# Strassen-style half-size products: sums of weight blocks by accumulating DMA instead of VectorE

## The chip, the core and the metric

The kernel runs on one core of one Trainium2 chip. The metric is the device time of one execution in microseconds; the median of three runs of the kernel before is 1508.66 us (1508.45 to 1508.77).

## What is computed

One layer of an encoder trunk on 512 rows of width 2048, all in float32. The input is normalised (RMS), multiplied by one large matrix `w_in` (2048 x 13312), and split into the operands of three mixers: a short gated convolution, a banded attention with eight heads and a cross-attention into 256 memory rows with four heads. Each mixer's output is gated, projected to 2048, weighted by a sigmoid gate, summed, and projected by `w_out`.

```python
h = rms_norm(x, norm_g); proj = h @ w_in
(a_b, a_c, a_x, a_z, q, k, v, b_z, mq, m_z, g_a, g_b, g_m) = split(proj)
ya = (a_b * conv3(a_c * a_x)) * silu(a_z) @ w_branch_a
yb = (band_attention(q, k, v) * silu(b_z)) @ w_branch_b
ym = (memory_attention(mq, mem_kv) * silu(m_z)) @ w_branch_m
merged = sigmoid(g_a + b0) * ya + sigmoid(g_b + b1) * yb + sigmoid(g_m + b2) * ym
out = x + merged @ w_out
```

## The kernel before, in words

**Products.** TensorE (PE) multiplies float32 data that were split into a rounded part `hi` and a remainder `lo` (type fp32r): a product is hi*hi + hi*lo + lo*hi. `split` (L182) makes the parts of a tile: ACT casts it to `hi`, then DVE subtracts to get `lo`.

**Pairs.** `pair` (L237) computes 512 rows x 1024 columns of `h @ w_in` or `merged @ w_out` by seven half-size products instead of eight (Winograd's form of Strassen's scheme). The inner dimension 2048 and the columns are halved, so the weight has blocks 11, 12, 21 and 22, and the left matrix has halves too. Products run in the order P1, P5, P6, P3, P7, P2, P4 (`ORDER`, L234); `LEFT` (L235) names the left operand of each, sums such as S1 and S2 that `Blocks.do` (L487) makes once for all pairs. There are 15 pairs: q, k, v, cx, bz, mqz, az, two for each of the gates ga, gb, gm, and two for `w_out` (o).

**Steps.** A product is cut into n = 4 steps, one for each raw tile of 128 x 2 x 512 values (512 KB) of the weight block: 12 matmuls of 512 columns. A pair has 28 steps. In `run_steps` (L123) step i issues, in this order: the loads of step i+6, the `adds` of step i, the split of step i+2, the matmuls of step i. That is the order of the instructions on each engine; when they really start is decided by the semaphores. Every wrapper `Engine` (L40) keeps its engine's instructions in the order written, and all show as line 48, so groups are read by tile names. Raw tiles come from a ring of 12; a load waits until its slot is free. `wst` holds three split tiles, so the cast for step i+2 waits for PE to have finished step i-1.

**Block sums before.** P5, P6, P7 and P4 need sums of weight blocks. The helper `sub` makes them on DVE in the raw tiles: 11 becomes 12-11, then 22-(12-11); 12 becomes 22-12; 21 becomes 21 minus the tile 11. Those are 16 subtractions of 128 x 1024 for each pair, 240 in all.

**Queues.** SP issues all weight loads and all stores of the pairs, in program order; a store that waits for its data holds back the loads behind it. ACT issues the loads of the attention heads. POOL computes the few square roots of the norms (`rstd_of`, L158) and issues no DMA.

Of the kernel before, what the change touches and what calls it, by code (L numbers as in the profile page):

```python
# [11 lines left out]
F32 = mybir.dt.float32  # L12
F32R = mybir.dt.float32r
AF = mybir.ActivationFunctionType
ALU = mybir.AluOpType
# [50 lines left out]
def trunk_layer(ctx: ExitStack, tc, x, mem, gx, gm, w_in, w_kv, bg, cw, hg, relz, w_a, w_b, w_m, w_o, out):  # L66
# [115 lines left out]
    def split(hi, lo, f):  # L182
        ACT.copy(hi, f)
        DVE.tensor_tensor(lo, f, hi.bitcast(F32), op=ALU.subtract)
# [52 lines left out]
    def pair(name, left, w, done, bias=None, addend=None):  # L237
# [6 lines left out]
        def loader(b, kh, nh, c):  # L244
            def fn():
                raw[b, c] = load(w(kh, nh, c), f"{name}_{b}{c}")
            return fn

        def sub(dst, a, b, c):
            return lambda: DVE.tensor_tensor(raw[dst, c], raw[a, c], raw[b, c], op=ALU.subtract)  # L250

        source = {"P1": "11", "P5": "11", "P6": "11", "P3": "22", "P7": "12", "P2": "21", "P4": "21"}
        key = {"P1": "X", "P5": "Z", "P6": "Y", "P3": "Z", "P7": "Y", "P2": "V", "P4": "Y"}

        def bias_of(i):
            return st8["bias"][i]

        def evac(p):
            b = ps[key[p]]
            new = lambda what: [cell(f"{what}_{name}{t}") for t in range(2)]  # L260
            if p == "P1":
                if bias is None:
                    cs["a"] = cs["b"] = new("pa")
                    for t in range(2):
                        ACT.copy(cs["a"][t], b[t])
                else:
                    cs["a"], cs["b"] = new("pa"), new("pb")
                    for t in range(2):
                        DVE.tensor_tensor(cs["a"][t], b[t], bias_of(0), op=ALU.add)
                        DVE.tensor_tensor(cs["b"][t], b[t], bias_of(1), op=ALU.add)  # L270
            if p == "P5":
                cs["f"] = new("pf")
                for t in range(2):
                    DVE.tensor_tensor(cs["f"][t], b[t], cs["b"][t], op=ALU.add)
            if p == "P6":
                cs["e"] = new("pe") if bias is None else cs["b"]
                for t in range(2):
                    DVE.tensor_tensor(cs["e"][t], b[t], cs["b"][t], op=ALU.add)
            if p == "P3":
                for t in range(2):  # L280
                    DVE.tensor_tensor(cs["e"][t], b[t], cs["e"][t], op=ALU.add)
                done(1, 0, cs["e"])
            if p == "P7":
                for t in range(2):
                    DVE.tensor_tensor(cs["f"][t], b[t], cs["f"][t], op=ALU.add)
                done(1, 2, cs["f"])
            if p == "P2":
                cs["g"] = new("pg")
                for t in range(2):
                    DVE.tensor_tensor(cs["g"][t], b[t], cs["a"][t], op=ALU.add)  # L290
                done(0, 0, cs["g"])
            if p == "P4":
                for t in range(2):
                    DVE.tensor_tensor(cs["a"][t], b[t], cs["a"][t], op=ALU.add)
                done(0, 2, cs["a"])

        for p in ORDER:
# [21 lines left out]

        for c in range(n):  # L320
            steps[s0 + c].loads.append(loader("11", 0, 0, c))
            steps[s0 + 1 + c].loads.append(loader("12", 0, 1, c))
            steps[s0 + 7 + c].loads.append(loader("22", 1, 1, c))
            steps[s0 + 19 + c].loads.append(loader("21", 1, 0, c))
            steps[s0 + c].adds.append(sub("11", "12", "11", c))
            steps[s0 + 5 + c].adds.append(sub("11", "22", "11", c))
            steps[s0 + (10, 12, 14, 16)[c]].adds.append(sub("12", "22", "12", c))
            steps[s0 + (20, 21, 22, 24)[c]].adds.append(sub("21", "21", "11", c))
        def add_last():
            for t, e in enumerate(addend()):  # L330
                DVE.tensor_tensor(cs["a"][t], cs["a"][t], e, op=ALU.add)
# [128 lines left out]
    class Blocks:  # L460
# [16 lines left out]
        def split(self, b, i, key):  # L477
            if b not in self.at:
                self.at[b] = [slot(n, f"{self.pre}{b}_{w}", (P, 8, MEM), F32R)
                              for n, w in zip(self.slots[b], ("hi", "lo"))]  # L480
            rows = slice(4 * i, 4 * i + 4)
            split(self.at[b][0][:, rows, :], self.at[b][1][:, rows, :], self.f(key, i))

        def combine(self, d, a, b, op, i):
            DVE.tensor_tensor(self.f(d, i), self.f(a, i), self.f(b, i), op=op)

        def do(self, what, i):  # L487
            if what == "s1":
                self.combine("S12", (0, 1), (1, 1), ALU.add, i)
            elif what == "s2":  # L490
                self.combine("S12", "S12", (0, 0), ALU.subtract, i)
            elif what == "s4":
                self.combine("S4", (1, 0), "S12", ALU.subtract, i)
            elif what == "s3":
                self.combine(self.s3, (0, 0), (0, 1), ALU.subtract, i)
            else:
                key = {"A11": (0, 0), "S1": "S12", "S2": "S12", "S4": "S4", "S3": self.s3, "A12": (1, 0), "A22": (1, 1)}
                self.split(what, i, key[what])
# [434 lines left out]
```

## Time and profile before

| what | value |
|---|---|
| median of 3 runs | 1508.66 us |
| the profiled execution: its own time | 1506.83 us |
| the profiled execution: span, first to last instruction | 1505.0 us |
| PE busy | 99% |
| DVE busy | 76% |
| ACT busy | 47% |
| POOL busy | 1% |
| DMA, mean over the span | 155 GB/s |

Times are of one execution; shares are of its span. PE's busy share counts pipelined matmuls whose ends are modelled. The granted clock was full (1.000) throughout, the 2.4 GHz level.

### The profile page before, as it was taken

What the parts mean: (1) busy time and instruction counts of PE and PEld (TensorE: products, weight loads), DVE (VectorE), ACT (ScalarE), POOL (GpSimd) and SP (SyncE); (2) the same over time, 40 slices, a digit from 0 to 9 for tenths busy, and PEclk for the clock granted to TensorE, in tenths of its full rate; (3) what the DMA queues carried; (4) which work ended last, traced back from release to release, by engine and by line L of the source; (5) the groups of instructions that cost most, each with busy time, mean ns of one, the idle gap of its engine ahead of it and who ended that gap; (6) DMA issues with size and microseconds to landing.
All of it is one profiled execution on the core that took longest, in us unless ns stands there. A gap on an engine that the chain in (4) does not pass through costs nothing.

```text
span 1505.0 us, 17896 instructions
## 1 busy us (share of the span) xinstructions
PE 1483.8 (99%) x6696; PEld 1200.1 (80%) x6696; DVE 1146.7 (76%) x1393; ACT 707.4 (47%) x1102; POOL 22.0 (1%) x23
## 2 busy tenths in 40 slices
PE   8999999999999999999999999999999999998998
PEld 4478888788888888888888888888887888886887
DVE  3887778677888778887877778787887464479977
ACT  3566666543445465444444444444445343354442
POOL 0000000000000000000000000000000000000000
PEclk9999999999999999999999999999999999999999
DMA  9525354363336253626446362543736666410724
GB/s 327 191 66 180 110 175 133 102 215 112 120 90 209 70 196 98 199 89 210 140 144 221 106 223 89 184 150 114 255 133 229 234 218 209 129 43 21 253 83 133
DMA packets 139190, 233.45 MB, mean 155 GB/s; under 512 B 9824, under 2 KB 35680, under 8 KB 138464
## 3 DMA queue, kind: packets, MB, share of 16 engines
q1 hardware_dynamic: 130320, 215.41, 43.7%
q10 hardware_dynamic: 8784, 16.91, 3.4%
q8 instruction: 52, 0.85, 0.2%
q14 instruction: 34, 0.28, 0.1%
HBM read 198.73 MB, written 36.17 MB: 156 GB/s over the span
## 4 chain that ended last, share of the span: by engine, by line
PE 90%; DVE 6%; ACT 1%; DMA 1%; issue 1%; POOL 0%; SPq 0%; DVEq 0%; ACTq 0%; POOLq 0%
PE ps_wb L48 6%; PE psY_gb L48 4%; PE psY_ga L48 4%; PE psY_o L48 4%; PE psY_gm L48 3%; PE ps_kv L48 3%; PE psZ_gm L48 3%; PE psZ_gb L48 3%; PE ps_wa L48 3%; PE ps_wm L48 3%; PE psZ_ga L48 3%; PE psY_k L48 2%; PE psY_cx L48 2%; PE psZ_o L48 2%; PE psY_mqz L48 2%; PE psY_bz L48 2%
## 5 line engine op out<-in xcount | busy, mean ns | idle before, releaser
L48 ACT CAST whi_o_P<-raw_o 128x1024 fp32r<-128x1024 f32 x56 | 58.8, 1054 | 85.1 <-PE psY_o L48 20.2
L48 DVE TENSOR_TENSOR wlo_gb_P<-raw_gb,whi_gb_P 128x1024 fp32r<-128x1024 f32 x56 | 68.2, 1223 | 31.7 <-ACT whi_gb_P L48 31.4
L48 DVE TENSOR_TENSOR wlo_ga_P<-raw_ga,whi_ga_P 128x1024 fp32r<-128x1024 f32 x56 | 68.2, 1223 | 30.9 <-ACT whi_ga_P L48 30.5
L48 DVE TENSOR_TENSOR wlo_gm_P<-raw_gm,whi_gm_P 128x1024 fp32r<-128x1024 f32 x56 | 68.4, 1223 | 23.2 <-ACT whi_gm_P L48 23.2
L48 DVE TENSOR_TENSOR wlo_o_P<-raw_o,whi_o_P 128x1024 fp32r<-128x1024 f32 x56 | 68.3, 1223 | 20.4 <-ACT whi_o_P L48 20.1
L48 ACT ACTIVATE p<-p,nm 128x128 f32<-128x128 f32 (+3 forms) x32 | 18.0, 564 | 107.5 <-DVE nm L48 100.9
L48 ACT CAST whi_gm_P<-raw_gm 128x1024 fp32r<-128x1024 f32 x56 | 58.7, 1051 | 20.8 <-PE psV_gm L48 5.0
L48 ACT CAST whi_ga_P<-raw_ga 128x1024 fp32r<-128x1024 f32 x56 | 58.2, 1049 | 11.4 <-PE psY_az L48 2.8
L48 ACT CAST whi_gb_P<-raw_gb 128x1024 fp32r<-128x1024 f32 x56 | 58.4, 1049 | 6.6 <-PE psY_gb L48 2.0
L48 ACT COPY p<-ptp 128x256 f32<-128x256 f32 (+3 forms) x48 | 19.6, 409 | 88.0 <-PE ptp L48 88.0
L48 PE MATMUL ps_kv<-raw_kv,mT 128*128 128x512 f32 x128 | 59.0, 615 | 1.0 <-DMA raw_kv<-in_w_kv 1.0
L48 PE MATMUL ps_wb<-whi_wb,yb_hi 128*128 128x512 f32 x128 | 50.1, 391 | 0.0
L48 PE MATMUL ps_wb<-whi_wb,yb_lo 128*128 128x512 f32 x128 | 49.8, 389 | 0.0
L48 PE MATMUL ps_wb<-wlo_wb,yb_hi 128*128 128x512 f32 x128 | 49.8, 389 | 0.0
L48 ACT CAST whi_cx_P<-raw_cx 128x1024 fp32r<-128x1024 f32 x28 | 29.5, 1055 | 42.9 <-PE psY_cx L48 13.2
L48 DVE TENSOR_TENSOR wlo_wb<-raw_wb,whi_wb 128x1024 fp32r<-128x1024 f32 x16 | 19.6, 1223 | 38.6 <-ACT whi_wb L48 38.6
L48 PEld LDWEIGHTS ps_kv<-raw_kv,mT 128*128 128x128 f32 x128 | 24.6, 198 | 29.3 <-issue 27.9
L48 DVE TENSOR_TENSOR wlo_cx_P<-raw_cx,whi_cx_P 128x1024 fp32r<-128x1024 f32 x28 | 34.3, 1224 | 17.6 <-ACT whi_cx_P L48 15.9
L48 DVE TENSOR_TENSOR wlo_mqz_P<-raw_mqz,whi_mqz_P 128x1024 fp32r<-128x1024 f32 x28 | 34.3, 1224 | 14.2 <-ACT whi_mqz_P L48 14.2
L48 DVE TENSOR_TENSOR wlo_v_P<-raw_v,whi_v_P 128x1024 fp32r<-128x1024 f32 x28 | 34.1, 1222 | 14.2 <-ACT whi_v_P L48 13.9
L48 ACT CAST whi_mqz_P<-raw_mqz 128x1024 fp32r<-128x1024 f32 x28 | 29.4, 1051 | 31.4 <-PE psZ_mqz L48 10.0
L48 ACT CAST whi_bz_P<-raw_bz 128x1024 fp32r<-128x1024 f32 x28 | 29.5, 1054 | 30.8 <-PE psZ_bz L48 7.7
(658 smaller groups left out, 4684.7 us busy)
## 6 DMA issues: line engine op xcount, KB each, us to landing
raw_ga<-in_w_in SPq DMA_DIRECT2D x32, 512.0 KB, 4.8
raw_gb<-in_w_in SPq DMA_DIRECT2D x32, 512.0 KB, 5.3
raw_gm<-in_w_in SPq DMA_DIRECT2D x32, 512.0 KB, 5.2
raw_o<-in_w_o SPq DMA_DIRECT2D x32, 512.0 KB, 6.2
raw_kv<-in_w_kv SPq DMA_DIRECT2D x16, 512.0 KB, 7.7
raw_q<-in_w_in SPq DMA_DIRECT2D x16, 512.0 KB, 3.8
raw_k<-in_w_in SPq DMA_DIRECT2D x16, 512.0 KB, 4.8
raw_v<-in_w_in SPq DMA_DIRECT2D x16, 512.0 KB, 4.6
```

Source lines behind the costliest of these rows:

```text
L48: ins = getattr(self.engine, op)(*args, **kwargs)
```

## The change

The block sums move from DVE to DMA. `plus` issues, from POOL's queue, a transfer of a weight block out of HBM that is added into the raw tile in SBUF (`accum_op=ALU.add`). Such a transfer can only add, so the algebra is written with plus signs: tile 11 becomes 11+12, then 11+12+22, and later 11+12+22+21 for P4; tile 12 becomes 12+22. To make up for the signs, S1, S2 and S3 are formed with the opposite sign, A22 is split with a factor of -1, and `evac` subtracts in two places. Blocks 12 and 22 are now first loaded for P7 and P3 alone: their loads move from steps 1 to 4 and 7 to 10 of the pair to steps 12 to 15 and 11 to 14. The 16 loads of each pair stay; 16 accumulating transfers of 512 KB come on top.

```diff
--- before.py
+++ after.py
@@ -246,10 +246,14 @@
                 raw[b, c] = load(w(kh, nh, c), f"{name}_{b}{c}")
             return fn
 
-        def sub(dst, a, b, c):
-            return lambda: DVE.tensor_tensor(raw[dst, c], raw[a, c], raw[b, c], op=ALU.subtract)
-
-        source = {"P1": "11", "P5": "11", "P6": "11", "P3": "22", "P7": "12", "P2": "21", "P4": "21"}
+        def plus(dst, kh, nh, c):
+
+            def fn():
+                src = w(kh, nh, c).rearrange("(k p) n -> p k n", p=P)
+                POOL.dma_start(raw[dst, c], src, accum_op=ALU.add)
+            return fn
+
+        source = {"P1": "11", "P5": "11", "P6": "11", "P3": "22", "P7": "12", "P2": "21", "P4": "11"}
         key = {"P1": "X", "P5": "Z", "P6": "Y", "P3": "Z", "P7": "Y", "P2": "V", "P4": "Y"}
 
         def bias_of(i):
@@ -267,15 +271,16 @@
                     cs["a"], cs["b"] = new("pa"), new("pb")
                     for t in range(2):
                         DVE.tensor_tensor(cs["a"][t], b[t], bias_of(0), op=ALU.add)
-                        DVE.tensor_tensor(cs["b"][t], b[t], bias_of(1), op=ALU.add)
+                        DVE.tensor_tensor(cs["b"][t], bias_of(1), b[t], op=ALU.subtract)
+            other, sign = (cs["a"], ALU.subtract) if bias is None else (cs["b"], ALU.add)
             if p == "P5":
                 cs["f"] = new("pf")
                 for t in range(2):
-                    DVE.tensor_tensor(cs["f"][t], b[t], cs["b"][t], op=ALU.add)
+                    DVE.tensor_tensor(cs["f"][t], b[t], other[t], op=sign)
             if p == "P6":
                 cs["e"] = new("pe") if bias is None else cs["b"]
                 for t in range(2):
-                    DVE.tensor_tensor(cs["e"][t], b[t], cs["b"][t], op=ALU.add)
+                    DVE.tensor_tensor(cs["e"][t], b[t], other[t], op=sign)
             if p == "P3":
                 for t in range(2):
                     DVE.tensor_tensor(cs["e"][t], b[t], cs["e"][t], op=ALU.add)
@@ -291,7 +296,7 @@
                 done(0, 0, cs["g"])
             if p == "P4":
                 for t in range(2):
-                    DVE.tensor_tensor(cs["a"][t], b[t], cs["a"][t], op=ALU.add)
+                    DVE.tensor_tensor(cs["a"][t], cs["a"][t], b[t], op=ALU.subtract)
                 done(0, 2, cs["a"])
 
         for p in ORDER:
@@ -319,13 +324,13 @@
 
         for c in range(n):
             steps[s0 + c].loads.append(loader("11", 0, 0, c))
-            steps[s0 + 1 + c].loads.append(loader("12", 0, 1, c))
-            steps[s0 + 7 + c].loads.append(loader("22", 1, 1, c))
+            steps[s0 + 12 + c].loads.append(loader("12", 0, 1, c))
+            steps[s0 + 11 + c].loads.append(loader("22", 1, 1, c))
             steps[s0 + 19 + c].loads.append(loader("21", 1, 0, c))
-            steps[s0 + c].adds.append(sub("11", "12", "11", c))
-            steps[s0 + 5 + c].adds.append(sub("11", "22", "11", c))
-            steps[s0 + (10, 12, 14, 16)[c]].adds.append(sub("12", "22", "12", c))
-            steps[s0 + (20, 21, 22, 24)[c]].adds.append(sub("21", "21", "11", c))
+            steps[s0 - 1 + c].adds.append(plus("11", 0, 1, c))
+            steps[s0 + 3 + c].adds.append(plus("11", 1, 1, c))
+            steps[s0 + 9 + c].adds.append(plus("12", 1, 1, c))
+            steps[s0 + 13 + c].adds.append(plus("11", 1, 0, c))
         def add_last():
             for t, e in enumerate(addend()):
                 DVE.tensor_tensor(cs["a"][t], cs["a"][t], e, op=ALU.add)
@@ -479,20 +484,26 @@
                 self.at[b] = [slot(n, f"{self.pre}{b}_{w}", (P, 8, MEM), F32R)
                               for n, w in zip(self.slots[b], ("hi", "lo"))]
             rows = slice(4 * i, 4 * i + 4)
-            split(self.at[b][0][:, rows, :], self.at[b][1][:, rows, :], self.f(key, i))
+            hi, lo, f = self.at[b][0][:, rows, :], self.at[b][1][:, rows, :], self.f(key, i)
+            if b != "A22":
+                split(hi, lo, f)
+                return
+
+            ACT.mul(hi, f, -1.0)
+            DVE.scalar_tensor_tensor(lo, f, -1.0, hi.bitcast(F32), ALU.mult, ALU.subtract)
 
         def combine(self, d, a, b, op, i):
             DVE.tensor_tensor(self.f(d, i), self.f(a, i), self.f(b, i), op=op)
 
         def do(self, what, i):
             if what == "s1":
-                self.combine("S12", (0, 1), (1, 1), ALU.add, i)
+                self.combine("S12", (0, 1), (1, 1), ALU.subtract, i)
             elif what == "s2":
-                self.combine("S12", "S12", (0, 0), ALU.subtract, i)
+                self.combine("S12", (0, 0), "S12", ALU.subtract, i)
             elif what == "s4":
                 self.combine("S4", (1, 0), "S12", ALU.subtract, i)
             elif what == "s3":
-                self.combine(self.s3, (0, 0), (0, 1), ALU.subtract, i)
+                self.combine(self.s3, (0, 1), (0, 0), ALU.subtract, i)
             else:
                 key = {"A11": (0, 0), "S1": "S12", "S2": "S12", "S4": "S4", "S3": self.s3, "A12": (1, 0), "A22": (1, 1)}
                 self.split(what, i, key[what])
```

**DVE, pair bz.** `wlo_bz_P_c` is the remainder of block c; the pair starts with P1. Before, from the first sum on:

```order
L48 TENSOR_TENSOR raw_bz_2975<-raw_bz_2994,raw_bz_2975 128x1024
L48 TENSOR_TENSOR wlo_bz_P_2_3117<-raw_bz_3022,whi_bz_P_2_3116 128x1024
L48 TENSOR_TENSOR raw_bz_2996<-raw_bz_3020,raw_bz_2996 128x1024
L48 TENSOR_TENSOR wlo_bz_P_3_3152<-raw_bz_3059,whi_bz_P_3_3151 128x1024
L48 TENSOR_TENSOR raw_bz_3022<-raw_bz_3057,raw_bz_3022 128x1024
L48 TENSOR_TENSOR wlo_bz_P_0_3171<-raw_bz_2975,whi_bz_P_0_3170 128x1024
L48 SCALAR_TENSOR_TENSOR cv_3186<-uT_3041,cw_sb,cv_3186 128x511
L48 SCALAR_TENSOR_TENSOR cv_3186<-uT_3041,cw_sb,cv_3186 128x510
```

and in the changed kernel, the same place:

```order
L48 TENSOR_TENSOR wlo_bz_P_2_3110<-raw_bz_3019,whi_bz_P_2_3109 128x1024
L48 TENSOR_TENSOR wlo_bz_P_3_3143<-raw_bz_3053,whi_bz_P_3_3142 128x1024
L48 TENSOR_TENSOR wlo_bz_P_0_3160<-raw_bz_2977,whi_bz_P_0_3159 128x1024
L48 SCALAR_TENSOR_TENSOR cv_3175<-uT_3037,cw_sb,cv_3175 128x511
L48 SCALAR_TENSOR_TENSOR cv_3175<-uT_3037,cw_sb,cv_3175 128x510
L48 TENSOR_TENSOR wlo_bz_P_1_3181<-raw_bz_2995,whi_bz_P_1_3180 128x1024
L48 TENSOR_TENSOR wlo_bz_P_2_3202<-raw_bz_3019,whi_bz_P_2_3201 128x1024
```

The sums `raw<-raw,raw` are gone from DVE; the remainders and the convolution's steps keep their order.

**POOL, from the roots of pair q to those of mqz.** Before, POOL has nothing but roots there:

```order
L48 TENSOR_TENSOR r_q_1549<-v_q_1547,mhalf 128x8
L48 TENSOR_TENSOR r_k_1737<-v_k_1735,mhalf 128x8
L48 TENSOR_TENSOR r_k_1936<-v_k_1934,mhalf 128x8
L48 TENSOR_TENSOR r_k_2134<-v_k_2132,mhalf 128x8
L48 TENSOR_TENSOR r_k_2323<-v_k_2321,mhalf 128x8
L48 TENSOR_TENSOR r_mq_4224<-v_mq_4222,mhalf 128x8
L48 TENSOR_TENSOR r_mq_4419<-v_mq_4417,mhalf 128x8
```

and in the changed kernel pair bz alone issues, between the roots of k and of mq, 16 transfers; these are the first twelve (three sets of four):

```order
L48 DMA raw_bz_2977<-in_w_in 128x2x512
L48 DMA raw_bz_2995<-in_w_in 128x2x512
L48 DMA raw_bz_3019<-in_w_in 128x2x512
L48 DMA raw_bz_3053<-in_w_in 128x2x512
L48 DMA raw_bz_2977<-in_w_in 128x2x512
L48 DMA raw_bz_2995<-in_w_in 128x2x512
L48 DMA raw_bz_3019<-in_w_in 128x2x512
L48 DMA raw_bz_3053<-in_w_in 128x2x512
L48 DMA raw_bz_3243<-in_w_in 128x2x512
L48 DMA raw_bz_3268<-in_w_in 128x2x512
L48 DMA raw_bz_3293<-in_w_in 128x2x512
L48 DMA raw_bz_3319<-in_w_in 128x2x512
```

Sets one and two go into the same four tiles (11), set three into the tiles 12, and a fourth set, not shown, into the tiles 11 again.

**SP, from the last stores of pair bz into pair mqz.** Before (`z_d` are stores of bz, `raw_mqz` loads of the next pair):

```order
L48 DMA z_d<-pg_bz_3610 128x4x128
L48 DMA z_d<-pg_bz_3611 128x4x128
L48 DMA raw_mqz_3663<-in_w_in 128x2x512
L48 DMA raw_mqz_3724<-in_w_in 128x2x512
L48 DMA z_d<-pa_bz_3209 128x4x128
L48 DMA z_d<-pa_bz_3210 128x4x128
L48 DMA raw_mqz_3745<-in_w_in 128x2x512
L48 DMA raw_mqz_3764<-in_w_in 128x2x512
L48 DMA raw_mqz_3787<-in_w_in 128x2x512
```

and in the changed kernel:

```order
L48 DMA z_d<-pg_bz_3609 128x4x128
L48 DMA z_d<-pg_bz_3610 128x4x128
L48 DMA z_d<-pa_bz_3196 128x4x128
L48 DMA z_d<-pa_bz_3197 128x4x128
L48 DMA raw_mqz_3793<-in_w_in 128x2x512
L48 DMA raw_mqz_3812<-in_w_in 128x2x512
L48 DMA raw_mqz_3814<-in_w_in 128x2x512
L48 DMA raw_mqz_3833<-in_w_in 128x2x512
L48 DMA raw_mqz_3835<-in_w_in 128x2x512
L48 DMA raw_mqz_3857<-in_w_in 128x2x512
L48 DMA raw_mqz_3859<-in_w_in 128x2x512
L48 DMA raw_mqz_3879<-in_w_in 128x2x512
```

Before, nine of the sixteen loads of mqz stand ahead of the last two stores of bz (two of the nine are shown here); now only four do, and the eight loads of blocks 22 and 12 stand in one row behind the last store of bz.

## Rows read from the trace of the kernel before

**Rows 1.** The page: busy time by engine; the DMA queue of SP: packets, MB, share.
```profile
PE 1483.8 (99%) x6696; PEld 1200.1 (80%) x6696; DVE 1146.7 (76%) x1393; ACT 707.4 (47%) x1102; POOL 22.0 (1%) x23
...
q1 hardware_dynamic: 130320, 215.41, 43.7%
```

**Rows 2.** The page: the chain that ended last, by engine.
```profile
PE 90%; DVE 6%; ACT 1%; DMA 1%; issue 1%; POOL 0%; SPq 0%; DVEq 0%; ACTq 0%; POOLq 0%
```

**Rows 3.** Waits of PE: what waited, for whom, us in total, times, longest.
```profile
PE psZ_o L48 <- DVE wlo_o_P L48: 4.4, 4, 1.7
PE psY_q L48 <- DVE wlo_q_P L48: 2.7, 1, 2.7
...
PE ps_wa L48 <- DVE wlo_wa L48: 0.9, 1, 0.9
PE psY_o L48 <- DVE wlo_o_P L48: 0.7, 1, 0.7
...
PE psZ_ga L48 <- DVE wlo_ga_P L48: 0.2, 1, 0.2
```

**Rows 4.** Waits of PE's weight loads, same columns.
```profile
PEld psZ_o L48 <- DVE wlo_o_P L48: 6.1, 4, 2.1
```

**Rows 5.** The chain in order of time, pair q: start us, us, what.
```profile
91.53 0.91 DVE raw_q L48
...
104.50 1.14 DVE raw_q L48
```

**Rows 6.** The chain in order of time, first w_out pair.
```profile
1342.46 0.81 DVE raw_o L48
...
1373.06 1.14 DVE raw_o L48
```

**Rows 7.** DVE groups: the sums of two pairs; count, busy us, mean ns, idle before.
```profile
L48 DVE TENSOR_TENSOR raw_gb<-raw_gb,raw_gb 128x1024 f32<-128x1024 f32 x32 | 38.9, 1216 | 0.0
...
L48 DVE TENSOR_TENSOR raw_bz<-raw_bz,raw_bz 128x1024 f32<-128x1024 f32 x16 | 19.5, 1220 | 0.0
```

**Rows 8.** Stretches: from:to, us, busy us of each engine, clock, DMA share, GB/s.
```profile
28.00:32.00 4.00, 3.89 (x14) 1.76 (x13) 2.80 (x10) 1.23 (x2) 0.56 (x1) 1.00 1.05 388
397.00:474.00 77.00, 77.00 (x346) 63.84 (x345) 68.84 (x73) 38.72 (x45) 0.00 (x0) 1.00 0.38 123
461.28:464.00 2.72, 2.72 (x13) 2.25 (x12) 2.42 (x3) 0.83 (x3) 0.00 (x0) 1.00 1.06 399
890.00:980.00 90.00, 90.00 (x429) 74.16 (x428) 69.27 (x95) 36.70 (x58) 0.00 (x0) 1.00 0.48 163
```

**Rows 9.** Tile raw_bz: its loads (issue ns, first and last start), and their landing.
```profile
L48 SPq DMA_DIRECT2D raw_bz<-in_w_in x16: 367/368/384, 363.0 to 438.2; - x16
...
DMA to landing us min/median/max: 3.5/4.4/5.0
```

**Rows 10.** POOL group: one of its rows of eight roots.
```profile
L48 POOL TENSOR_TENSOR r_k<-v_k,mhalf 128x8 f32<-128x8 f32 x4 | 6.5, 1636 | 87.3 <-DVE v_k L48 87.3
```

**Rows 11.** Timeline of ACT, pair bz, first cast of P5: start us, us, operation.
```profile
403.27 1.06 ACT L48 CAST whi_bz_P<-raw_bz 128x1024 fp32r<-128x1024 f32 x1 [1.07 <-issue]
```

**Rows 12.** Timeline of DVE, pair bz, the remainder of that tile.
```profile
404.51 1.22 DVE L48 TENSOR_TENSOR wlo_bz_P<-raw_bz,whi_bz_P 128x1024 fp32r<-128x1024 f32 x1
```

**Rows 13.** The chain in order of time, pairs bz and mqz.
```profile
408.63 10.88 PE psZ_bz L48 x48
...
473.91 10.88 PE psX_mqz L48 x48
484.79 10.88 PE psZ_mqz L48 x48
495.67 10.88 PE psY_mqz L48 x48
```

**Rows 14.** Timeline of SP's queue, start of pair mqz.
```profile
475.56 0.97 SPq L48 DMA_DIRECT2D z_d<-pa_bz  x2
476.58 1.82 SPq L48 DMA_DIRECT2D raw_mqz<-in_w_in  x3
```

## The prediction

> **What bounds the kernel now.** I read the page first. PE is busy 99% of the span, DVE 76%, POOL 1%, and SP's DMA queue holds the DMA engines 43.7% of it [rows 1]. The chain that ended last lies on PE for 90% and on DVE for 6% [rows 2]: PE is the bound, and DVE work counts only where PE waited for it. The waits of PE say where: eight groups name DVE's remainders, from 4.4 us in the w_out pairs and 2.7 us in pair q down to 0.2 us in ga, 10.2 us in all with the 0.9 us at the first step of w_branch_a [rows 3]. PE's weight loads saw more, 6.1 us where PE's own row has 4.4 [rows 4]. So what DVE could give back is small against 1500 us, and what matters as much is whether the new transfers arrive before PE needs them. For that I read the stretches (how full DMA is in a pair), the timelines of one pair (when a split tile is ready and when PE takes it) and SP's queue.
>
> **What is removed.** 240 sums on DVE: 32 for each of ga, gb, gm and o, 16 for each of seven pairs, 1.22 us each [rows 7], 293 us of DVE's 1146.7. On the path that sets the end lie few of them. In pair q the chain runs over four sums, 0.91 us for the first and 1.14 us for the last [rows 5], together 4.3 us where PE waited 2.7; in the first w_out pair over eight, 0.81 us to 1.14 us [rows 6], together 8.9 us where PE waited 5.1. Each is more than the wait beside it, so these waits should go, if nothing is late in their place. I count 11 us: the 10.2 us of PE and a little of what the weight loads show. What is late next is the split itself, ACT's cast and DVE's remainder, 1.06 and 1.22 us for each step [rows 11, 12], which fit in a step of 10.88/4 = 2.72 us [rows 13]. The moved signs exchange subtractions for additions of the same size and cost nothing; A22's remainder gets another DVE form, four times, in place of the lighter load, and is hidden by the sums gone. PE itself is not slowed by full DMA engines: in a slice with DMA share 1.06 it still did 13 matmuls in 2.72 us [rows 8].
>
> **What is added: the price of one transfer.** The trace has no accumulating DMA and no DMA from POOL, so its price is bounded. With the engines full, DMA moved 388 GB/s [rows 8]: a plain 512 KB load (524288 bytes) holds all engines 1.35 us. That is the lower end: the addition is free and the tile need not be read. The upper end counts three passes, reading the addend, reading the tile and writing it, each as one plain transfer: 4.05 us. I take 2.7 us: a plain row already contains one read and one write, and the addition brings one more read, of the tile. What comes on top: the fastest plain load landed 3.5 us after its issue [rows 9], so 3.5 - 1.35 = 2.15 us are fixed; for the issue POOL may need between 0.37 us, as SP does [rows 9], and 1.64 us, as for its own eight roots [rows 10]; I take the latter, since this is also work that POOL has to do by itself. Alone, a sum then lands 6.5 us after its tile is free; the ends are 3.9 and 7.8.
>
> The Trainium skill, Collectives: The Full Stack, "The bandwidth ceiling: the fold count and why AG ≠ RS ≠ AR", states that an add in the DMA engine needs two source reads in the same ring, and gives a measured ratio of 1.93 to the copy; no run here shows it yet. By that ratio the price would be an estimated 2.6 us and the sum below would end some 6 us lower.
>
> **Do they fit in the mean?** Pair bz moves 123 GB/s for 77 us, 9.5 MB, 24.4 us at 388 GB/s [rows 8]; 16 sums at 2.7 us add 43.2: 67.6 of 77 us. A gate pair has 163 GB/s for 90 us, 37.8 + 43.2 = 81 of 90 us [rows 8]. So DMA is not the bound, but nearly full.
>
> **Do they arrive in time?** The first two sets work on the tiles that are just in use: the tile is split for P1, then a sum, then split for P5, a second sum, then P6, four steps apart. In bz the first remainder of P5 is done at 404.51 + 1.22 = 405.73, 2.9 us before P5 begins at 408.63 [rows 12, 13]. Put on mqz, where P1, P5 and P6 begin at 473.91, 484.79 and 495.67 [rows 13]: the eight sums are released from 471.0 on, every 2.72 us, the last at 490.0. The last tile must have landed 1.06 + 1.22 = 2.28 us before P6's last step at 495.67 + 3 x 2.72 = 503.83, at 501.6. Undisturbed, each takes 2.7 us of engine time and keeps the pace. But SP's last stores of the pair before go out at 475.56, and only from 476.6 [rows 14] the eight loads of blocks 22 and 12 follow, all at once: their slots are long free, and the order shows them in one row behind these stores. By then one and a half sums are through (two issued, starting at 472.6). The other 6.5 share the engines with the loads; if the queues take turns row by row, each passes with one load, in 2.7 + 1.35 = 4.05 us: 26.3 us, done at 502.9, landed at 505.1, 3.5 us after 501.6. PE waits 3.5 us, once a pair. The other pairs hold the loads behind stores in the same way. I count nine (q, k, v, cx, bz, mqz, az, both o), 31.5 us. A gate pair has 90/28 = 3.2 us a step, which moves the limit 11 x 0.5 = 5.3 us later than the release of the loads, so the six gate pairs wait for nothing. Sets three and four have five and nine steps and are hidden. POOL's roots stand in the same queue as the transfers; 240 issues of 1.64 us are 394 us on an engine busy 22 us, hidden too, unless a root stands behind a waiting transfer; DVE waits for the root, and the remainders for DVE.
>
> **Sum.** -11 + 31.5 = +20.5 us. The profiled execution took 1506.83 us and would take 1527.3; the median of the runs shown is 1.83 us above it, so 1529 us. By the price of the sums: at 1.35 us the last tile lands at 476.6 + 6.5 x 2.7 + 2.15 = 496.3, in time.
>
> **Rivals.**
> - **The sums arrive in time; the kernel is faster.** Deciding point: 501.6 - 2.15 - 476.6 = 22.9 us for 6.5 sums, 3.5 us each with its load, so a price up to 2.17 us. For it: reading the tile may overlap with reading HBM, or loads and sums may not take turns evenly, and 3.5 us is little against my uncertain 1.64. Against it: the tile must be read. Time: 1508.66 - 11 = 1497.7, from 1493 (all that the weight loads saw comes back) to 1505.
> - **No change to be seen.** At about 2.4 us the wait is 6.5 x 0.23 = 1.5 us in nine pairs, 13 us, against 11 gained; or the change does not do what it says on PE, because the splits still come late from ACT. Time: 1505.6 to 1511.7.
> - **DMA becomes the bound.** At 4.05 us, three passes, bz needs 24.4 + 64.8 = 89.2 of 77 us and a gate pair 37.8 + 64.8 = 102.6 of 90: 12.4 us more for each of 15 pairs, 186 us, about 1690. The deciding point is (77 - 24.4)/16 = 3.3 us a sum. For it: 388 GB/s was seen for loads alone, and nothing shows how the engines add. [...]
>
> **How the numbers follow.** The forecast, sums late in the pairs with short steps (1512 to 1600), has 0.38: my price is the one nearest to a known row plus one read. In time: 0.36, since the limit of 2.17 us is close. No change: 0.11. DMA bound: 0.15. A measurement of this kernel tells 0.2%, some 3 us, from no change. So faster 0.36, within 0.2% 0.11, slower 0.53. Both signs hold much chance; the forecast's own range is 1512 to 1600. The whole range reaches from 1494, nearly all of the faster case, to 1605; beyond it lies most of the DMA-bound case and a little at the lower end, 0.17 in all.
>
> **What would show it.** Right: a queue of POOL with some 126 MB in the DMA table; DVE 293 us less busy; no DVE wait in q and o; but ACT's casts of P5 and P6 waiting for DMA into raw tiles, PE waiting for remainders in cx, bz, mqz and az, where it now never waits, and not in the gate pairs. Landing of sums above 10 us at the start of a pair and near 6.5 later. Wrong towards faster: sums landing in 8 us or less even beside the eight loads. Wrong towards much slower: DMA share near 1.0 throughout the pairs, and steps longer in the gate pairs too. If DVE waits for POOL grow in q and k, the roots behind the transfers are the cause, which I count at nothing.

## The result and the profile after

The changed kernel takes 1593.35 us (1590.68 to 1595.35, four runs, as many as of the kernel before) where the kernel before takes 1508.66: a ratio of 1.0562, 95% interval 1.0548 to 1.0577, 84.7 us slower. The forecast was slower, by 20.5 us. The whole range holds the time, and so does the forecast's own range of 1512 to 1600; the size is four times what the sum gave. The profiled execution spans 1588.9 us.

The page of the changed kernel (engines, the two large DMA queues, the chain by engine), beside [rows 1] and [rows 2]:

```profile
PE 1517.4 (96%) x6696; PEld 1205.2 (76%) x6696; DVE 886.5 (56%) x1153; ACT 706.3 (44%) x1102; POOL 313.5 (20%) x263
...
q0 software_dynamic: 65280, 125.84, 44.1%
q1 hardware_dynamic: 130320, 215.41, 40.6%
...
PE 47%; DMA 20%; issue 19%; POOL 5%; DVE 5%; ACT 3%; SPq 1%; POOLq 0%; ACTq 0%; DVEq 0%
```

DVE has 240 instructions fewer and is busy 260 us less, where 293 was forecast. POOL's queue q0 is new, 240 transfers that hold 44.1% of sixteen engines' span: 0.441 x 1588.9 / 240 = 2.92 us each, beside the forecast's 2.7. The chain lay 90% on PE; now less than half of it does, and DMA (20%) and time for which the profile shows no wait ("issue", 19%) have taken its place.

The waits of PE, beside [rows 3]: the waits of q and o for DVE are still there under the same names, and cx, mqz, bz, az and gb, which never waited, now do. The two longest are of another kind: one for a cast on ACT (`whi_v_P`) and one for a load of the attention (`yb_in`).

```profile
PE psZ_v L48 <- ACT whi_v_P L48: 7.2, 1, 7.2
PE pt_yb L48 <- DMA yb_in<-yo_d: 5.3, 1, 5.3
...
PE psZ_k L48 <- DVE wlo_k_P L48: 4.5, 1, 4.5
PE psY_q L48 <- DVE wlo_q_P L48: 4.4, 3, 2.9
PE psY_mqz L48 <- DVE wlo_mqz_P L48: 3.0, 4, 0.8
PE psY_o L48 <- DVE wlo_o_P L48: 3.0, 4, 0.8
PE psY_cx L48 <- DVE wlo_cx_P L48: 3.0, 4, 0.8
```

A remainder on DVE waits for its cast on ACT, and the cast for the sum. So the timeline of ACT at the start of pair mqz is the place to look. Between P5's third tile and P6's last:

```profile
526.27 1.06 ACT L48 CAST whi_mqz_P<-raw_mqz 128x1024 fp32r<-128x1024 f32 x1 [2.13 <-DMA raw_mqz<-in_w_in]
530.26 1.05 ACT L48 CAST whi_mqz_P<-raw_mqz 128x1024 fp32r<-128x1024 f32 x1 [2.93 <-DMA raw_mqz<-in_w_in]
534.30 1.05 ACT L48 CAST whi_mqz_P<-raw_mqz 128x1024 fp32r<-128x1024 f32 x1 [2.99 <-DMA raw_mqz<-in_w_in]
...
542.31 1.05 ACT L48 CAST whi_mqz_P<-raw_mqz 128x1024 fp32r<-128x1024 f32 x1 [2.99 <-DMA raw_mqz<-in_w_in]
546.27 2.94 ACT L48 CAST whi_mqz_P<-raw_mqz 128x1024 fp32r<-128x1024 f32 x3 [2.90 <-DMA raw_mqz<-in_w_in]
```

A cast comes every 4.0 us, each after an idle time that a transfer into the raw tile ends; PE wants one every 2.72 us. The 4.0 us are the 4.05 us that the prediction gives to a sum and a load that take turns. SP's queue in the same pair, and the DMA share in that stretch (columns as in [rows 8]):

```profile
514.28 1.10 SPq L48 DMA_DIRECT2D z_d<-pa_bz  x2
515.47 41.42 SPq L48 DMA_DIRECT2D raw_mqz<-in_w_in  x12
```

```profile
523.40:549.50 26.10, 22.36 (x90) 16.14 (x89) 9.47 (x9) 8.80 (x9) 7.28 (x6) 1.00 1.10 262
```

As forecast, eight loads go out in one row behind the last stores, from 515.47 on. The line merges twelve: the last four, block 21's, follow only from 549.74 on, when the eight sums have landed. POOL's queue shows something that the prediction had not: it does not issue every sum when its tile is free. Its sixth issue in the pair, at 526.51, comes as the sum issued at 516.74 lands (the cast of 526.27 waited for that one); those of 518.16 and 520.88 are still open:

```profile
510.00 1.20 POOL L48 DMA_DIRECT2D raw_mqz<-in_w_in  x1 [21.94 <-DVE wlo_mqz_P L48]
512.67 1.22 POOL L48 DMA_DIRECT2D raw_mqz<-in_w_in  x1 [1.48 <-DVE wlo_mqz_P L48]
516.74 1.21 POOL L48 DMA_DIRECT2D raw_mqz<-in_w_in  x1 [2.84 <-DVE wlo_mqz_P L48]
518.16 1.20 POOL L48 DMA_DIRECT2D raw_mqz<-in_w_in  x1 [0.20 <-issue]
520.88 1.21 POOL L48 DMA_DIRECT2D raw_mqz<-in_w_in  x1 [1.51 <-DVE wlo_mqz_P L48]
526.51 1.22 POOL L48 DMA_DIRECT2D raw_mqz<-in_w_in  x1 [4.42 <-DMA raw_mqz<-in_w_in]
...
DMA to landing us min/median/max: 5.6/11.6/13.3
```

Before any experiment, then, there were these theories. **A:** the price. A sum costs the DMA engines about two plain transfers, and where sums meet loads they come too late: A1 says that this is a matter of the place where the loads stand, A2 of how full the engines are over the whole pair. Two more came with the later runs: D joins these two (how full a pair is, and where its loads stand), and E says that sets 1 and 2 have too little time wherever the loads stand. **B:** POOL's queue itself, its issues of 1.2 us and the roots behind them. **C:** the few sums that POOL may have open at once. Where a pair loses was read, for every run, from the start of its P1 to the start of the next pair's, minus the same of the kernel before (the last to the end of the span; ga, gb, gm and o are two pairs each). Of these, q varies without a wait of its own: in late_sets and in the two kernels at the end it is 1.6 to 1.9 us longer while PE waits there as long as before (2.7 to 2.9 us), and the granted clock from 107 to 110 us is 0.52 to 0.60, where the kernel before has 1.00.

```
pair   before   after  plain  early  late_   tight_  tight_sets_  set_1_  first_
                                     sets    sets    early        early   out_two_sets
q        81.5     6.5   -1.8    2.4    1.9     6.7       4.0        6.0     1.6
k        81.2     9.9   -1.2   -0.9   -0.2     3.5      -0.9       -0.1     0.0
v        80.8    11.8    4.4    8.7    5.2     3.8       2.2        0.5     0.0
cx       77.1     6.9    0.0    2.1    0.0     7.1       1.9        1.8     0.0
bz       77.0     4.2    0.0    0.0    0.0     3.5       0.0        0.1     0.0
mqz      76.2     6.1    0.0    1.6    0.0     6.6       1.3        0.9     0.0
az       79.2     2.8   -0.3   -0.3    0.1     3.2      -0.3        0.9     0.0
ga      179.4     6.8   -0.5   -0.5    0.0     5.4      -0.5       -0.5     0.0
gb      179.2    13.4    0.2    8.0    0.0    12.5       6.7        2.0     0.0
gm      352.1    12.4    0.7    8.9   -0.8     6.3       8.0        0.0     0.0
o       165.2     3.6   -4.9    1.1   -0.2     3.6       0.2       -0.7    -4.4
```

The nine pairs of the forecast lost 51.8 us, the six gate pairs 32.6.

### The profile page after: what moved, and what is told of

Its sections match the earlier page's. It is cut to its first block, busy times and chain, and to the rows that moved or that the text cites. A ratio compares the mean times of both kernels' runs of the same rounds, so it can differ in the third digit from the quotient of the medians.

```text
span 1588.9 us, 18387 instructions
## 1 busy us (share of the span) xinstructions
PE 1517.4 (96%) x6696; PEld 1205.2 (76%) x6696; DVE 886.5 (56%) x1153; ACT 706.3 (44%) x1102; POOL 313.5 (20%) x263
## 3 DMA queue, kind: packets, MB, share of 16 engines
q0 software_dynamic: 65280, 125.84, 44.1%
## 4 chain that ended last, share of the span: by engine, by line
PE 47%; DMA 20%; issue 19%; POOL 5%; DVE 5%; ACT 3%; SPq 1%; POOLq 0%; ACTq 0%; DVEq 0%
PE ps_wb L48 5%; PE ps_wa L48 3%; PE ps_wm L48 3%; DMA raw_o<-in_w_o 2%; PE ps_kv L48 2%; PE psY_gm L48 2%; DMA raw_gb<-in_w_in 2%; DMA raw_ga<-in_w_in 2%; DMA raw_mqz<-in_w_in 2%; PE psY_q L48 2%; PE psZ_gm L48 2%; PE psY_o L48 2%; PE psY_mqz L48 2%; PE psY_cx L48 2%; DMA yb_in<-yo_d 1%
## 5 line engine op out<-in xcount | busy, mean ns | idle before, releaser
L48 POOL DMA_DIRECT2D raw_o<-in_w_o x32 | 38.8, 1226 | 303.8 <-DVE wlo_o_P L48 262.4
L48 POOL DMA_DIRECT2D raw_gm<-in_w_in x32 | 38.8, 1258 | 155.5 <-DVE wlo_gm_P L48 50.1
L48 POOL DMA_DIRECT2D raw_gb<-in_w_in x32 | 38.8, 1217 | 150.4 <-DVE wlo_gb_P L48 56.4
L48 POOL DMA_DIRECT2D raw_ga<-in_w_in x32 | 38.8, 1226 | 135.4 <-DVE rs L48 31.7
L48 DVE TENSOR_TENSOR wlo_q_P<-raw_q,whi_q_P 128x1024 fp32r<-128x1024 f32 x28 | 34.2, 1225 | 33.4 <-ACT whi_q_P L48 33.4
L48 DVE TENSOR_TENSOR wlo_k_P<-raw_k,whi_k_P 128x1024 fp32r<-128x1024 f32 x28 | 34.2, 1225 | 32.3 <-ACT whi_k_P L48 32.3
L48 DVE TENSOR_TENSOR wlo_az_P<-raw_az,whi_az_P 128x1024 fp32r<-128x1024 f32 x28 | 34.1, 1224 | 30.6 <-ACT whi_az_P L48 30.4
```

The source lines that it names most:

```text
L48: ins = getattr(self.engine, op)(*args, **kwargs)
```

## The experiments

Edits are shown against the changed kernel, written out where the kernels choose by a switch; "..." marks what is left out. The kernel before took 1507.47 us beside plain, early, late_sets and tight_sets, 1508.19 beside half_room, double_room, signs_only and first_out, and 1507.20 beside tight_sets_early, set_1_early and first_out_two_sets.

**plain: the transfers without the addition.**

```diff
-                POOL.dma_start(raw[dst, c], src, accum_op=ALU.add)
+                POOL.dma_start(raw[dst, c], src)
```

> This kernel keeps every transfer of POOL's queue, its size and its place, but leaves out the addition: a transfer overwrites the raw tile, so 240 sums of the reference's computation are missing. Theory A (the addition's price: a sum holds the DMA engines 2.7 us instead of 1.35 us, and sums and loads that meet then go 4.05 us a pair): POOL's queue falls from 44.1% of the span to about 1.35 x 240 / 1500 = 22%, sum and load that meet go 2.7 us a pair, one step, and the time falls to 1495 to 1515 us. Theory B (POOL's queue itself: its issues, the few transfers that it lets stand open, the roots behind them): these stay, and the time stays above 1560 us.

Measured: 1505.29 us (ratio 0.9987, 0.9977 to 0.9996). The whole loss is gone. Queue, chain and landings of pair mqz:

```profile
q0 software_dynamic: 34560, 125.84, 23.3%
...
PE 91%; DMA 4%; DVE 2%; issue 1%; ACT 1%; SPq 0%; POOL 0%; ACTq 0%; DVEq 0%; POOLq 0%
```

```profile
L48 POOL DMA_DIRECT2D raw_mqz<-in_w_in x16: 722/722/731, 474.4 to 509.4; - x16
...
DMA to landing us min/median/max: 3.8/7.7/10.0
```

The same bytes out of HBM, the same places, the same queue: 144 packets for a transfer instead of 272, 0.233 x 1503.3 / 240 = 1.46 us of sixteen engines instead of 2.92, an issue of 0.72 us instead of 1.2. Without the addition the loss is gone: theory A. (The shorter issue and the number of open transfers change with it; the latter is tried below.) The 4.4 us left in v are not POOL's queue: ACT waits there for a small store of the attention, and PE for ACT's cast behind it. The chain has that store, and under it the same store in the kernel before:

```profile
275.55 6.31 DMA qk_d<-qt_k
```

```profile
277.10 2.39 DMA qk_d<-qt_k
```

**early: all sums on DMA, blocks 12 and 22 loaded where the kernel before loads them.**

```diff
-            steps[s0 + 12 + c].loads.append(loader("12", 0, 1, c))
-            steps[s0 + 11 + c].loads.append(loader("22", 1, 1, c))
+            steps[s0 + 1 + c].loads.append(loader("12", 0, 1, c))
+            steps[s0 + 7 + c].loads.append(loader("22", 1, 1, c))
```

> All sums stay on DMA; the loads of blocks 12 and 22 go back to the places that they have in the kernel before (steps 1 to 4 and 7 to 10). Theory A1 (the meeting of loads and sums at the pair's start is what costs): of the twelve loads behind the last stores about five go out before them, so five meetings of 1.35 us in fifteen pairs are saved, up to 100 us if all stood on the path, more likely half: 1530 to 1555 us. Theory A2 (the engines are full over the whole pair, the place of a load does not matter): 1580 to 1600 us. Theory B (POOL's queue): no load stands in it, so 1580 to 1600 us too.

Measured: 1538.65 us (1.0202, 1.0187 to 1.0217): 31.2 us slower than before, where the change is 84.7. Not one transfer fewer, and 54 us come back. SP's row of loads behind pair bz's last stores has seven transfers now, not twelve, and three of them, not eight, go out at once. When these have passed, POOL's timeline in pair mqz shows sums alone, one every 2.55 us:

```profile
507.23 1.20 POOL L48 DMA_DIRECT2D raw_mqz<-in_w_in  x1 [1.44 <-DVE wlo_mqz_P L48]
509.77 1.20 POOL L48 DMA_DIRECT2D raw_mqz<-in_w_in  x1 [1.34 <-issue]
512.34 1.22 POOL L48 DMA_DIRECT2D raw_mqz<-in_w_in  x1 [1.37 <-issue]
514.87 1.21 POOL L48 DMA_DIRECT2D raw_mqz<-in_w_in  x1 [1.30 <-issue]
```

That is the price of a sum, and it lies under PE's step of 2.72 us, which is why the pair comes through. Theory A1, though 31.2 us remain. A2 falls: the engines are as good as full in every pair, and pair bz (first row) loses nothing by it; gb (second row) does.

```profile
409.00:486.00 77.00, 77.00 (x345) 63.87 (x344) 51.89 (x57) 38.81 (x45) 19.37 (x16) 1.00 0.99 232
821.60:1008.80 187.20, 182.64 (x852) 147.22 (x850) 103.87 (x162) 74.57 (x111) 39.03 (x33) 1.00 0.94 244
```

**late_sets and tight_sets: which sets cost.** A set on DVE is an addition of two raw tiles at the place of the old subtraction; the first kernel has sets 1 and 2 there and early loads, the second sets 3 and 4 with the loads of the changed kernel.

```diff
+        def on_dve(dst, src, c):
+            return lambda: DVE.tensor_tensor(raw[dst, c], raw[dst, c], raw[src, c], op=ALU.add)
...
-            steps[s0 - 1 + c].adds.append(plus("11", 0, 1, c))
-            steps[s0 + 3 + c].adds.append(plus("11", 1, 1, c))
+            steps[s0 + c].adds.append(on_dve("11", "12", c))
+            steps[s0 + 5 + c].adds.append(on_dve("11", "22", c))
```

```diff
-            steps[s0 + 9 + c].adds.append(plus("12", 1, 1, c))
-            steps[s0 + 13 + c].adds.append(plus("11", 1, 0, c))
+            steps[s0 + (10, 12, 14, 16)[c]].adds.append(on_dve("12", "22", c))
+            steps[s0 + (20, 21, 22, 24)[c]].adds.append(on_dve("11", "21", c))
```

> Sets 1 and 2 are DVE sums again, sets 3 and 4 stay on DMA; blocks 12 and 22 are loaded at the places of the kernel before, since DVE needs them as tiles. Theory A1 (sets 1 and 2 meet the loads with no room): all of the loss goes, 1503 to 1515 us, and DVE's waits in q and in the first w_out pair are back. Theory A2 (the mean load of the DMA engines): half the transfers, half the loss, 1540 to 1560 us. Theory B (POOL's queue): half the issues, and the roots stand behind fewer transfers, 1520 to 1550 us.

> Sets 1 and 2 stay on DMA, sets 3 and 4 are DVE sums; the loads stand as in the changed kernel. Theory A1 (sets 1 and 2 meet the loads): most of the loss stays, 1550 to 1590 us, and the gate pairs lose less, since nothing follows behind. Theory A2 (mean load): half the loss, 1540 to 1560 us. If all four sets share the loss by what follows them (sets 3 and 4 keep the engines full behind 1 and 2), this kernel and the one with sets 3 and 4 alone together explain less than the whole 84.7 us.

Measured: 1512.68 us (1.0034, 1.0023 to 1.0045) for sets 3 and 4 alone, 1569.13 (1.0402, 1.0384 to 1.0419) for sets 1 and 2 alone: 5.2 and 61.7 us, together 66.9 of 84.7. Sets 1 and 2 make most of the loss, sets 3 and 4 by themselves little. The two kernels differ in the loads too: with early loads sets 1 and 2 cost 23 us (tight_sets_early below). The table tells what sets 3 and 4 add beside the first two: k 6.4, v 8.0, gm 6.1 us. In the changed kernel the longest wait of PE in each of the three stands behind a transfer of the attention that went out among the sums (two stores of 256 KB and a load of 1 MB): 4.5 us in k, 7.2 in v, 5.3 in gm, and none of these is among PE's waits with sets 1 and 2 alone. The chain, in that order:

```profile
195.38 14.46 DMA qk_d<-qt_q
...
295.43 10.41 DMA qk_d<-qt_k
...
1170.62 22.16 DMA yb_in<-yo_d
```

In the kernel before the first took 2.3 us, the second 2.39, and the two loads of `yb_in` 4.9 and 6.9 us.

Alone, sets 3 and 4 cost 5.2 us in v, and what PE waits for is not a sum but the same small store. The timeline of ACT there, then the chain:

```profile
285.35 0.69 ACT L48 ACTIVATE qt_k<-pq_k,hg_sb 128x512 f32<-128x512 f32 x1 [6.07 <-DMA qk_d<-qt_k]
```

```profile
278.37 6.90 DMA qk_d<-qt_k
```

ACT waits 6.07 us for the store to give its buffer back; the store took 6.90 us between the sums. Behind that wait stands the cast that PE needs.

**half_room and double_room: the sums that POOL may have open.**

```diff
-dynamic_dma_scratch_size=2048
+dynamic_dma_scratch_size=1024
```

```diff
-dynamic_dma_scratch_size=2048
+dynamic_dma_scratch_size=4096
...
-    junk = cst.tile([P, S], mybir.dt.bfloat16, name="junk")
+    junk = cst.tile([P, S], mybir.dt.float8e4, name="junk")
-    sml = ctx.enter_context(tc.tile_pool(name="sml", bufs=3))
+    sml = ctx.enter_context(tc.tile_pool(name="sml", bufs=2))
```

> The changed kernel with half the memory for POOL's DMA descriptors (1024 instead of 2048 bytes a partition), nothing else. The trace of the changed kernel shows an issue waiting for the landing of the third sum before it. Theory A (the DMA engines are the limit where sums and loads meet): fewer sums stand open, each lands sooner, the step of 4.0 us between two sums stays, the time stays within 10 us of 1593. Theory C (the few sums that POOL may have open are the limit): one or two open sums of some 6 us and more each, 1630 us and above.

> The changed kernel with twice the memory for POOL's DMA descriptors (4096 bytes a partition; to make room, a scratch tile that nothing reads has a narrower type and a pool of small tiles two buffers in place of three). Theory A (the engines are the limit): sums are issued earlier and land later by as much, the step of 4.0 us stays, within 10 us of 1593. Theory C (the open sums are the limit): 1560 us or less, and POOL's roots, which no longer stand behind a waiting issue, give back the waits of pairs k and v, some 10 us of it.

Measured: 2064.99 us (1.3694, 1.3674 to 1.3713) with half, 1591.77 us (1.0558, 1.0544 to 1.0573) with double. With half the room POOL has one sum open at a time; it then lands in 5.7 us (median, 5.5 the fastest), and the next is issued behind it, every 6.0 us:

```profile
723.16 1.21 POOL L48 DMA_DIRECT2D raw_mqz<-in_w_in  x1 [4.59 <-issue]
729.11 1.22 POOL L48 DMA_DIRECT2D raw_mqz<-in_w_in  x1 [4.74 <-issue]
```

So the limit is real, and it decides when it is small; theory A's expectation for it, within 10 us of 1593, failed. The changed kernel's three are enough: with double the room, where up to seven stand open, the sums of mqz go out earlier and land by as much later, and nothing is gained, not in k and v either (9.7 and 14.3 us lost, where the change lost 9.9 and 11.8). Landings of raw_mqz in the table of DMA issues, median last, first the changed kernel, then double room:

```profile
raw_mqz<-in_w_in POOLq DMA_DIRECT2D x16, 512.0 KB, 11.6
```

```profile
raw_mqz<-in_w_in POOLq DMA_DIRECT2D x16, 512.0 KB, 13.4
```

Theory C falls for the change as it stands, and the part of B that lays k's and v's loss on roots held up by waiting issues falls with it. The changed kernel's trace says the same directly: DVE waits for the roots of q and k as long as before (7.2 us each there).

```profile
DVE t_k L48 <- POOL r_k L48: 7.2, 4, 1.8
DVE t_q L48 <- POOL r_q L48: 7.1, 4, 1.8
```

**signs_only: all sums on DVE, with the new signs and the old loads.** All four sets as in the two diffs above, none by `plus`.

> All 240 sums on DVE with the new signs, loads at the places of the kernel before: the part of the change that is not DMA. If signs and A22's other DVE form cost nothing, within 0.2% of the kernel before: 1504.5 to 1510.5 us; if they cost something, above 1511 us.

Measured: 1507.95 us (0.9998, 0.9989 to 1.0007). The moved signs and A22's other form cost nothing, as the prediction said.

**tight_sets_early and set_1_early: is it the window or the fill?** Sets 1 and 2, or set 1 alone, by DMA, the others on DVE, the loads as in `early`. For the first kernel:

```diff
-            steps[s0 + 12 + c].loads.append(loader("12", 0, 1, c))
-            steps[s0 + 11 + c].loads.append(loader("22", 1, 1, c))
+            steps[s0 + 1 + c].loads.append(loader("12", 0, 1, c))
+            steps[s0 + 7 + c].loads.append(loader("22", 1, 1, c))
...
-            steps[s0 + 9 + c].adds.append(plus("12", 1, 1, c))
-            steps[s0 + 13 + c].adds.append(plus("11", 1, 0, c))
+            steps[s0 + (10, 12, 14, 16)[c]].adds.append(on_dve("12", "22", c))
+            steps[s0 + (20, 21, 22, 24)[c]].adds.append(on_dve("11", "21", c))
```

> Sets 1 and 2 by DMA as in the run with sets 1 and 2 alone, sets 3 and 4 on DVE, but the loads of blocks 12 and 22 at the places of the kernel before. With all four sets and these loads the DMA engines had a share of 0.94 to 1.02 in every pair, and gb and gm still lost 8.0 and 8.9 us. Theory D (how full the engines are in a pair decides, and where the loads stand): with half the sums a gate pair is at 0.48 + 0.26 = 0.74, nothing is lost in ga, gb and gm, and the whole comes to 1503 to 1513 us. Theory E (sets 1 and 2 have too little time wherever the loads stand): gb and gm keep 5 us each and more, 1520 us and above.

> Only set 1 by DMA in every pair (60 sums), all others on DVE, loads at the places of the kernel before. Theory D: nothing is lost but the attention stores in v that come late beside sums, 0 to 4 us, and the first w_out pair gains 2.5 us as in the run of that set alone: 1504 to 1509 us. Theory E: half of what sets 1 and 2 lose, 1512 us and above.

Measured: 1530.25 us (1.0151, 1.0138 to 1.0165) and 1517.46 us (1.0064, 1.0048 to 1.0079): 23 and 10 us slower. Theory D falls; the ranges of E came in, though not in every pair (k, bz, az and ga lose nothing). Over the whole of gb the DMA share is 0.71, and the pair still loses 6.7 us. In the stretch where the eight sums of its first pair fall, the engines are full all the same (first 16 us, then the next, then the one behind):

```profile
816.00:832.00 16.00, 16.00 (x77) 12.98 (x76) 10.60 (x16) 5.90 (x9) 4.84 (x4) 1.00 1.00 256
832.00:848.00 16.00, 15.07 (x70) 11.37 (x69) 6.53 (x11) 4.86 (x7) 3.64 (x3) 1.00 1.11 250
848.00:864.00 16.00, 14.92 (x68) 11.76 (x67) 12.20 (x19) 7.86 (x12) 0.00 (x0) 1.00 0.22 62
```

Besides eight sums and eight loads, the attention's own transfers stand in them, on ACT's queue:

```profile
824.89 0.50 ACTq L48 DMA_DIRECT2D bias<-skew  x1
...
833.55 0.47 ACTq L48 DMA_DIRECT2D z<-z_d  x1
```

Their part in it was not tried by itself. Set 1 alone loses mostly in q (6.0 us): there the chain of waits runs from a sum of set 1 that lands after 12.27 us to its cast, and from there over DVE's remainders, POOL's root and a sum of set 2 (on DVE) to P6. PE waits 2.4 us more there than in the kernel before. From 110 to 116 us the granted clock is 0.50, the 1.2 GHz level, after PE had done nothing from 107 to 110; what it costs (an estimate: half of the 5.4 us that PE was busy then) is most of the rest of the 6.0 us.

**first_out and first_out_two_sets: DMA only where DVE is late.** All sums on DVE and early loads, but the first w_out pair has set 1 by DMA (four sums), or sets 1 and 2 (eight). Against `signs_only`, for set 1 (the pair's name is o0):

```diff
-            steps[s0 + c].adds.append(on_dve("11", "12", c))
+            if name == "o0":
+                steps[s0 - 1 + c].adds.append(plus("11", 0, 1, c))
+            else:
+                steps[s0 + c].adds.append(on_dve("11", "12", c))
```

> As the kernel with all sums on DVE and new signs, but the first set of the first w_out pair (four sums) goes by DMA: there PE waits 4.4 us for DVE's remainders in the kernel before, and the run without addition shows these two pairs 4.9 us shorter. Theory A: four sums alone meet four to eight loads at most and have 10.9 us: the wait goes, 1502 to 1505 us. Rival: the loads of this pair stand as close as in the others and the landing of 10 us and more makes PE wait 3 to 4 us in place of the DVE wait: 1507 to 1512 us.

> As the run with the first set of the first w_out pair by DMA, and its second set too (eight sums in all). In that run PE still waits 1.9 us for remainders of P5 and 0.7 us for one of P6, and DVE has four sums of set 2 in the chain. Gain theory: another 1 to 2 us, 1503 to 1505.5 us. Rival: eight sums meet the pair's twelve loads at the end of the pair before and P6 waits for them: 1506 to 1510 us.

Measured: 1505.83 us (0.9983, 0.9974 to 0.9991), just above what the gain theory gave, then 1503.81 us (0.9975, 0.9965 to 0.9985) for eight sums, as expected: 3.4 us faster than the kernel before, a small gain, but clear of the noise. PE's waits for P5's remainders in w_out, 4.4 us in [rows 3], became, with four and with eight sums:

```profile
PE psZ_o L48 <- DVE wlo_o_P L48: 1.9, 2, 1.5
```

```profile
PE psZ_o L48 <- DVE wlo_o_P L48: 0.7, 2, 0.4
```

## Why the prediction was right in direction and wrong in size

- **What bounds the kernel: right.** PE was the bound, DVE counted only where PE waited, and 240 sums off DVE gave little: some 8 us in the run without addition (q 1.8, where PE's wait fell from 2.7 to 0.8; k 1.2; o 4.9), where the prediction put 11, and v's 4.4 us against it. In the changed kernel not even that: PE's waits in q and o stayed.
- **The price: right.** 2.7 us was taken, 2.55 us is what sums alone take, 4.0 us with a load against 4.05. The Trainium skill, Collectives: The Full Stack, "The bandwidth ceiling: the fold count and why AG ≠ RS ≠ AR", states that an add needs two source reads and gives a measured ratio of 1.93 to the copy. The ratio agrees with this kernel's runs: 272 packets to 144 is 1.89, and 2.92 to 1.46 us is 2.0; that two reads are the reason, no run here shows.
- **Which sums collide: right in kind, mis-sized.** In mqz the first two sums landed at 515.6 and 518.3, in 5.6 and 5.7 us, as if alone; the loads went out at 515.47, so "one and a half sums are through" was about right. The third was issued 4.07 us after the second, not 2.72, since ACT did two activations of the pair before ahead of its cast; it landed at 526.2, and the other five followed every 4.0 us. The last landed at 546.17, 33.7 us after P1 began at 512.5, where 31.2 was forecast (505.1 - 473.91) and 27.7 is the limit (501.6 - 473.91). The wait is 6.0 us instead of 3.5, and the pair is 6.1 us longer. The run with sets 1 and 2 alone, which is what this step describes, loses 38.0 us in the nine pairs, what DVE gave back there already taken off, where -11 + 31.5 = 20.5 was forecast: too small by 17.5 us, but not the largest error.
- **"The six gate pairs wait for nothing": wrong, and the largest error.** 24.2 us in that run, 32.6 with all sets. The forecast left them 1.8 us (28.5 us of sums from the loads on, 30.3 to the limit). In the second gb pair the loads went out at 960.76 and the last sum of the eight landed at 997.24, 36.5 us later: the first sum landed 3.5 us after the loads began (in mqz 0.1 us), the second and third took 5.5 and 7.5 us more, with the attention's transfers beside them, and the last five 4.0 us each. A term with so thin a margin should have been given half a chance, not zero. In gm, 5.3 of the 12.4 us with all sets are the wait for `yb_in`, not for a sum.
- **"Sets three and four have five and nine steps and are hidden": right as sums, wrong in what they hold up.** 5.2 us alone, but some 22 us more than the run of sets 1 and 2 when they follow behind sums that are already late, and 8 us with the loads moved forward (1.0202 against 1.0151). 17.0 us of PE's waits in k, v and gm stand behind the attention's own transfers, which the prediction did not count.
- **The miss in one sum.** By the table, 24.2 us (gate pairs) + 17.5 (the nine others) + 22.2 (sets 3 and 4 on top) = 63.9, of the 64.2 between 84.7 and 20.5. That the forecast's own range still held the time is its width, not its mechanism.
- **"Nearly full": too low.** For bz the prediction had 67.6 of 77 us; `early`, with the same transfers, shows a share of 0.99 there. The 24.4 us of the other traffic were worked out from 388 GB/s, though the same row said 0.38 x 77 = 29.3 us [rows 8]; with 16 sums at 2.92 that is 76 us. The share of the row should have been used, not its bytes. Full was not yet the bound: bz lost nothing by it.
- **POOL's roots, "which I count at nothing": right.** The sign that was named, DVE waiting longer for POOL in q and k, did not come (7.1 and 7.2 us, before 7.2 each). The loss of k and v beyond the late sums went over the two small stores.
- **The clock was left out.** The kernel before has a granted clock of 1.00 up to its last instructions. The changed kernel has five stretches at 0.50 (the 1.2 GHz level), in q, k, v, gb and gm; PE was busy for some 23 us of them, so about half of that, 11 to 12 us (an estimate), is part of the losses above. In v the clock was 0.50 in the stretch from 304 us, after PE had been busy 2.43 of the 6 us ahead of it, and 0.82 from 310 to 320.

```profile
298.00:304.00 6.00, 2.43 (x11) 1.68 (x9) 0.00 (x0) 0.00 (x0) 2.16 (x3) 0.95 1.11 225
304.00:310.00 6.00, 1.95 (x4) 1.25 (x5) 1.98 (x2) 3.99 (x12) 1.91 (x2) 0.50 1.12 233
```

Of the rivals, "the sums arrive in time" came in exactly when the addition was taken out (1505.29, at the end of its 1493 to 1505); "no change" did not happen. "DMA becomes the bound" did not come at its price of 4.05 us, but much of its sign did: the DMA share was 0.88 to 1.00 in the pairs of the changed kernel, and the gate pairs were longer.

## What to carry to other kernels

An accumulating DMA that takes work off an engine which is not the bound buys only the waits for that engine, and here it was paid for with twice the DMA time of a plain transfer: count it by what else is in flight in the few microseconds in which it must land, not by the mean over the stage, and ask which transfers of other work will stand among the new ones. Look first at what the same change moves into that window: here putting two rows of loads back was worth 54 of 85 us. The profitable form was small: eight sums of 240, at the place where PE waited longest for DVE and the DMA engines had room (a share of 0.02 from 1335 to 1375 us in the kernel before; each of the eight landed in 5.9 to 6.7 us).

## What the runs showed of the hardware that was not expected

- An accumulating 512 KB transfer takes 272 packets where a plain one takes 144, holds POOL for 1.2 us instead of 0.72 us to issue, and alone lands in 5.5 to 5.7 us; the fastest plain one from the same queue landed in 3.8 us.
- The memory for POOL's descriptors sets how many such transfers stand open: one at 1024 bytes a partition (6.0 us from one to the next), three at 2048, up to seven at 4096. Beyond three more room gave nothing here.
- Full DMA engines showed in other transfers too: stores of 256 KB took 6.90 to 14.46 us instead of 2.3 to 2.4, and held up ACT or DVE, not the tile that everybody was watching.
